# Context keys and values in 512-column products, with the two halves added afterwards

## The chip, the cores and the metric

The kernel runs on one core of one Trainium2 chip. The metric is the device time of one execution in microseconds (us), lower is better. Before the change three runs took 632.14, 632.98 and 632.99 us, median 632.98 us.

## The reference, cut to what matters

One layer: x (1024 tokens by 1024) and a context of 256 tokens by 1024 are normalised and modulated to h and hc. h is multiplied by an input projection of 4096 columns, split into queries, keys, values and gates of an attention half (8 heads of 64) and the parts of a convolution half. Of the context only keys and values are wanted:

```python
kc, vc = jnp.split(hc @ w_in[:, D_ATTN:3 * D_ATTN], 2, axis=-1)
kc = rmsnorm(heads(kc), k_norm_g)
vc = heads(vc)
attn = neighbourhood_attention(q, k, heads(v), kc, vc, rpb) * jax.nn.silu(za)
```

Everything is float32. Both halves are gated, joined, sent through an output projection and added to x.

## The kernel before, in words

To keep precision, each operand of a large product is split into a high part (rounded to the fast matmul type fp32r) and a low part (the rest), and one product becomes three: high by high, high by low, low by high. `mm3` issues these three matmuls into one PSUM accumulator. Tiles that end in h or l, or index 0 and 1, are these parts.

The program has four stages: a start (to about 77 us) that norms and transposes x and the context and makes the first conv columns; the projection of queries, keys and values (to about 267 us); the attention with the other gates' and the conv's products as fillers; and the output projection.

The change lies in the second stage. The loop over n runs over 4 pairs of heads (p) times 8 token tiles (t), with a tail. For a pair, eight chunks of w_in (128 rows by three times 128 columns: the pair's query, key and value columns) are loaded by SyncE (SP) (`chunk_load`) and split (`chunk_split`: ScalarE, ACT, rounds the high part, VectorE, DVE, subtracts for the low part). `proj_tile` multiplies a token tile by the eight chunks, 24 matmuls of 384 columns, into one of four PSUM banks (`pacc`). A step n then runs the later steps of earlier tiles: the root-mean-square scale of tile n-1 (`head_scale`: a square on ACT, a sum on DVE, a power on POOL), its values (`put_v`), then the norm (`normed`, tiles `qn`) and rotary turn (`rotated`, tiles `rot` and `rtmp`) of tile n-2, and the transposes on TensorE (PE) of a pair of tiles (`turn_qk`, tiles `trA` and `trB`).

Once per pair, `ctx_products` multiplies the two context tiles by the key and value columns of the same eight chunks (256 columns), at t = 2 for the first three pairs and at t = 0 for the last. Its two accumulators (`cacc`) take both banks of the PSUM tag U, which the gate and conv units (`pu`) and the gate row (`pgate`) use too. One step later `head_scale` reads them on ACT (`sq<-cacc`), two steps later `normed_ctx` norms the keys (`kn`) and stores the values (`vs<-cacc`), and `turn_kc` transposes the keys (`trC`).

In this stage every engine and SP's queue work strictly in the order of the code: an instruction that waits holds up all that is behind it on its engine. `rtmp` is one buffer (bufs=1).

Of the kernel before, what the change touches and what calls it, by code (L numbers as in the profile page):

```python
# [10 lines left out]
F32 = mybir.dt.float32  # L11
F32R = mybir.dt.float32r
BF16 = mybir.dt.bfloat16
AF = mybir.ActivationFunctionType
ALU = mybir.AluOpType
# [4 lines left out]
P = 128  # L20
# [3 lines left out]
KT = D // P  # L24
# [15 lines left out]
def body(tc, es, x, ctxt, w_ada, b_ada, w_in, q_g, k_g, rpbr, w_out, vecs, cst, out):  # L40
# [21 lines left out]
    pe, act, dve, pool = every = [ordered(e) for e in (nc.tensor, nc.scalar, nc.vector, nc.gpsimd)]  # L62
    sp = ordered(nc.sync)

    def sbuf(name, side=None, bufs=1):
        kw = {} if side is None else {"side": side}
        return tc.tile_pool(name=name, bufs=bufs, reuse_waits="tile", **kw)
# [4 lines left out]
    def mm3(ps, ah, al, bh, bl, first, last):  # L72

        i = pe.matmul(ps, ah, bh, start=first, stop=False)  # L74
        pe.matmul(ps, ah, bl, start=False, stop=False)  # L75
        pe.matmul(ps, al, bh, start=False, stop=last)  # L76
        return i
# [84 lines left out]
    def chunk_load(col, k):  # L162
        raw = wpp.tile([P, 3, P], F32, name="wr", tag="wr", bufs=5)
        chunk_anchor[:] = [sp.dma_start(raw, bass.AP(w_in.tensor, w_in.offset + (k * P) * 4096 + col,
                                                     [[4096, P], [512, 3], [1, P]]))]
        return raw

    def chunk_split(raw):
        raw = raw[:].rearrange("p a b -> p (a b)")
        wh = wpp.tile([P, 384], F32R, name="wh", tag="wh", bufs=12)  # L170
        wl = wpp.tile([P, 384], F32R, name="wl", tag="wl", bufs=12)
        act.copy(wh, raw)
        dve.tensor_tensor(wl, raw, wh[:].bitcast(F32), ALU.subtract)
        return wh, wl

    def load_chunk(col, k):
        return chunk_split(chunk_load(col, k))

    def head_scale(pp, ps, n):

        act.activation(sq[:, :n, :HD], by_head(ps[:, :n * HD]), AF.Square, scale=0.125)
        ss = pp.tile([P, 4], F32, name="ss", tag="ss", bufs=7)
        dve.tensor_reduce(ss[:, :n], sq[:, :n], AX.X, ALU.add)
        pool.tensor_tensor(ss[:, :n], ss[:, :n], mhalf[:, :n], ALU.pow)
        return ss

    def by_head(v):
        return v.rearrange("p (h d) -> p h d", d=HD)
# [7 lines left out]
    def next_vs():  # L196
        vss.append(vss.pop(0))
        return vss[-1]
# [4 lines left out]
    def put_v(vs, i, ps):  # L203

        halves(vs[:, :, 0, i, :HD], vs[:, :, 1, i, :HD], ps.rearrange("p (s d) -> p s d", s=2))
# [50 lines left out]
    def ctx_products(ch):  # L256

        acc = [psm.tile([P, 512], F32, name="cacc", tag="U", bufs=2) for _ in range(2)]
        for k in range(KT):
            wh, wl = ch[k]  # L260
            for i in range(2):
                hk = hc[k // 4][:, k % 4, :, i * P:(i + 1) * P]
                mm3(acc[i][:, :256], hk[:, 0], hk[:, 1],
                    wh[:, P:384], wl[:, P:384], k == 0, k == KT - 1)
        return acc

    def normed_ctx(pp, acc, scales):
        two, vs = [], next_vs()
        for i in range(2):
            qn = pp.tile([P, P], F32, name="kn", tag="kn", bufs=2)  # L270
            normed(qn, acc[i], scales[i], 2)
            pool.tensor_tensor(by_head(qn[:]), by_head(qn[:]), gkc.broadcast_to([P, 2, HD]), ALU.mult)
            put_v(vs, i, acc[i][:, P:256])
            two.append(qn)
        return two, vs
# [13 lines left out]
    def proj_tile(ch, t):  # L289
        ps = bank("pacc", "OOSS"[t % 4])  # L290
        for k in range(KT):
            wh, wl = ch[k]
            mm3(ps[:, :384], hh[k][:, t * P:(t + 1) * P], hl[k][:, t * P:(t + 1) * P], wh, wl, k == 0, k == KT - 1)
        return ps


    def unit_load(col):
        raws = []
        for q in range(2):
            raws.append(uw.tile([P, 4, P], F32, name="uraw", tag="uraw", bufs=2))  # L300
            sp.dma_start(raws[q], w_in[0, q * 512:(q + 1) * 512, col:col + P].rearrange("(k p) n -> p k n", p=P))
        return raws
# [84 lines left out]
    def z_col(f):  # L387
        return CZA + f * P if f < 4 else CZC + (f - 4) * P
# [135 lines left out]
    wpp = wps.enter_context(sbuf("wpp"))  # L524
# [10 lines left out]
    xx, slabs, highs, lows, chunks, mods, pts = {}, {}, {}, {}, {}, {}, {}  # L535
# [171 lines left out]

    def first_columns(half, k, part=range(3)):

        wh, wl = chunks[k]  # L710
        h_, l_ = (v.rearrange("p (b r c) -> p b (r c)", b=8, r=16)[:, :, 64 * half:64 * half + 64]
                  for v in (hh[k], hl[k]))
        for i in part:
            for u in (0, 2, 1):
                uc = slice(u * P, (u + 1) * P)
                pe.matmul(acc0[u][half], (wl if i == 1 else wh)[:, uc], l_ if i == 2 else h_,
                          start=k == 0 and i == 0, stop=k == KT - 1 and i == 2)
# [35 lines left out]
    def split_chunk(k):  # L753
        chunks[k] = chunk_split(chunks[k])
# [70 lines left out]
    for m in range(1, 4):  # L825
        k, new, last = 2 * m, m < 3, m == 3
# [4 lines left out]
        if m == 2:  # L831
            gkc = gains(tables)
            ch = [chunk_load(CQ, k) for k in range(4)]
# [82 lines left out]
    def bank(name, tag):  # L916
        return (pss if tag == "S" else psm).tile([P, 512], F32, name=name, tag=tag, bufs=2)
# [285 lines left out]
    pp = pps.enter_context(sbuf("ppn"))  # L1203
# [12 lines left out]
    def flush():  # L1216
        while stores:
            stores.pop(0)()

    for n in range(NT + 3):  # L1220


        p, t = divmod(n, NB)
        at = 2 if p < NPAIR - 1 else 0
        if 1 <= t and p + 1 < NPAIR:
            raws += [chunk_load(CQ + (p + 1) * P, k) for k in ([t - 1] if t < NB - 1 else [t - 1, t])]
        if n == 0:
            loaded[z_col(4)] = unit_load(z_col(4))
        if n == NT - 8:
            loaded[z_col(0)] = unit_load(z_col(0))  # L1230
        if 1 <= n <= KT:
            gate.load(n - 1)
            next(spread, None)
        if 9 <= n < 25 and n % 2:
            next(tables)
        if n == NT - 3:
            act.activation(few[:, 5:6], ones, AF.Exp)
        if n == NT - 6:
            heads[0].masks()
            heads[0].load_k()  # L1240
        if n == NT - 5:
            heads[0].load_q()
        flush()

        if t == 0 and 0 < n < NT:
            nxt += map(chunk_split, raws)
            ch, nxt, raws = nxt, [], []
        if n == 0:
            next(group0)
        if n == NT - 4:  # L1250
            next(fill)
        if n < NT:
            tiles[n] = proj_tile(ch, t)
        else:
            for _ in range((4, 3, 1)[n - NT]):
                next(fill)
        if 5 <= n < 9:
            for _ in range(2):
                next(group0)
        if n == 9:  # L1260
            for _ in group0:
                pass
        if 0 < n <= NT:
            scales[n - 1] = head_scale(pp, tiles[n - 1], 4)
            if n % 2:
                vs = next_vs()
            put_v(vs, (n - 1) % 2, tiles[n - 1][:, 256:384])
            if n % 2 == 0:
                q, r = divmod(n - 1, NB)
                spill_v(q, r - 1, vs)  # L1270
        if t == at + 1 and n < NT:
            cscales = [head_scale(pp, a, 2) for a in cacc]

        if 1 < n <= NT + 1:
            m, r = n - 2, (n - 2) % NB
            qn = rms_normed(pp, tiles[m], scales.pop(m))
        while waiting:
            waiting.pop(0)()
        if 4 <= t and p + 1 < NPAIR:
            nxt.append(chunk_split(raws.pop(0)))  # L1280
        if 1 < n <= NT + 1:
            tiles[m] = rotated(pp, rope, qn, r)
        if t == at + 2 and n < NT:
            kc = normed_ctx(pp, cacc, cscales)
        do_dves()
        if 2 <= n < KT + 2:
            gate.add(n - 2)
        if 9 <= n < 25 and n % 2 == 0:
            next(tables)
        do_acts()  # L1290

        if n == KT + 3:
            gate.split()
        if n == KT + 5:
            gate.sum()
        if t == at and n < NT:
            cacc = ctx_products(ch)
        if n % 2 == 0 and n >= 4:
            waiting.append(turn_qk(pp, (n - 4) // NB, [tiles.pop(n - 4), tiles.pop(n - 3)], (n - 4) % NB))
        if t == at + 3 and n < NT:  # L1300
            waiting.append(turn_kc(pp, p, *kc))
# [43 lines left out]
    with sbuf("att") as ap, psum("psb") as psb:  # L1345
# [6 lines left out]
        for n in range(4 * NH + 4):  # L1352
# [8 lines left out]
            if ready:  # L1361
                p = ready.pop()
# [153 lines left out]
```

## Time and profile before

| what | value |
|---|---|
| median of three runs | 632.98 us |
| the profiled execution | 632.67 us |
| its span, first to last recorded instruction | 630.9 us |
| PE busy | 624.0 us, 3504 matmuls |
| DVE, ACT busy | 436.8 us, 327.7 us |
| PE in the chain that ended last | 96% |
| products of the context (`cacc`) in that chain | 4% |

The time of the profiled execution is 1.8 us above its span; that rest lies before the first and behind the last recorded instruction. Matmuls overlap in the records, so what a stream of them costs is read from the distance of their starts, which the chain of work shows as the length of a piece over its count, and not from the duration of one.

### The profile page before, as it was taken

What the parts mean: (1) busy time and instruction counts of PE and PEld (TensorE: products, weight loads), DVE (VectorE), ACT (ScalarE), POOL (GpSimd) and SP (SyncE); (2) the same over time, 40 slices, a digit from 0 to 9 for tenths busy, and PEclk for the clock granted to TensorE, in tenths of its full rate; (3) what the DMA queues carried; (4) which work ended last, traced back from release to release, by engine and by line L of the source; (5) the groups of instructions that cost most, each with busy time, mean ns of one, the idle gap of its engine ahead of it and who ended that gap; (6) DMA issues with size and microseconds to landing.
All of it is one profiled execution on the core that took longest, in us unless ns stands there. A gap on an engine that the chain in (4) does not pass through costs nothing.

```text
span 630.9 us, 10022 instructions
## 1 busy us (share of the span) xinstructions
PE 624.0 (99%) x3504; PEld 540.3 (86%) x3504; DVE 436.8 (69%) x866; ACT 327.7 (52%) x705; POOL 77.6 (12%) x102
## 2 busy tenths in 40 slices
PE   8999999999999999999999999999999999999998
PEld 3577899999999999888888888888888888888887
DVE  1887858766856755468888889987998865594211
ACT  4776935424625446346676568567775854460000
POOL 1305014123123222000000000000000002003300
PEclk9999999999999999999999999999999999999999
DMA  8983638866775994975383636673742234962721
GB/s 320 368 284 106 178 114 261 262 199 211 267 244 164 298 330 142 322 230 188 124 290 104 227 94 214 192 272 104 275 124 74 60 101 149 361 210 88 261 101 50
DMA packets 103006, 125.60 MB, mean 199 GB/s; under 512 B 9665, under 2 KB 71577, under 8 KB 101676
## 3 DMA queue, kind: packets, MB, share of 16 engines
q1 hardware_dynamic: 96492, 113.38, 54.4%
q10 hardware_dynamic: 6208, 11.05, 5.5%
q8 instruction: 27, 0.44, 0.3%
q0 software_dynamic: 256, 0.54, 0.3%
q14 instruction: 23, 0.19, 0.1%
HBM read 88.09 MB, written 38.62 MB: 201 GB/s over the span
## 4 chain that ended last, share of the span: by engine, by line
PE 96%; DMA 1%; DVE 1%; SPq 1%; issue 0%; ACT 0%; ACTq 0%
PE pu L55 30%; PE pacc L55 21%; PE po L55 8%; PE acc L55 5%; PE pout L76 5%; PE pout L75 5%; PE pout L74 5%; PE cacc L55 4%; PE tr L55 4%; PE pss L55 3%; PE pmx L55 2%; PE pc L55 2%; DMA xx<-in_x 1%; PE trA L55 1%; PE trB L55 1%
## 5 line engine op out<-in xcount | busy, mean ns | idle before, releaser
L55 PE MATMUL pu<-h,uh 128*128 128x512 f32 x544 | 169.4, 392 | 0.6 <-DVE cv L55 0.6
L55 PE MATMUL pacc<-wh,h 128*128 128x384 f32 x512 | 135.1, 338 | 0.0
L55 PEld LDWEIGHTS pu<-h,uh 128*128 128x128 f32 x544 | 98.1, 188 | 18.2 <-DVE cv L55 1.0
L55 PE MATMUL pu<-h,ul 128*128 128x512 f32 x272 | 106.4, 391 | 0.0
L55 PEld LDWEIGHTS pacc<-wh,h 128*128 128x128 f32 x512 | 92.9, 188 | 0.1
L55 PE MATMUL pacc<-wl,h 128*128 128x384 f32 x256 | 85.6, 334 | 0.0
L55 PEld LDWEIGHTS pu<-h,ul 128*128 128x128 f32 x272 | 51.1, 188 | 11.3
L55 POOL TENSOR_TENSOR ss<-ss,few 128x4 f32<-128x4 f32 (+1 forms) x40 | 41.5, 1038 | 125.2 <-DVE ss L55 125.0
L75 PE MATMUL pout<-wol,yh 128*128 128x512 f32 (+2 forms) x136 | 51.6, 379 | 0.0
L74 PE MATMUL pout<-woh,yh 128*128 128x512 f32 (+2 forms) x136 | 50.5, 379 | 0.0
L76 PE MATMUL pout<-woh,yl 128*128 128x512 f32 (+2 forms) x136 | 49.8, 379 | 0.0
L55 PEld LDWEIGHTS pacc<-wl,h 128*128 128x128 f32 x256 | 48.1, 188 | 0.1
L55 DVE TENSOR_REDUCE ss<-sq 128x4 f32<-128x260 f32 (+1 forms) x40 | 15.7, 393 | 40.6 <-ACT sq L55 40.6
L55 ACT ACTIVATE sq<-pacc 128x256 f32<-128x256 f32 x32 | 12.3, 385 | 52.7 <-PE pacc L55 52.2
L55 DVE TENSOR_REDUCE rm<-pmx 128x2 f32<-128x256 f32 x32 | 13.6, 424 | 30.4 <-PE pmx L55 30.2
L55 DVE TENSOR_TENSOR mx<-mx,sb 128x384 f32<-128x384 f32 (+1 forms) x64 | 33.0, 524 | 2.0
L55 ACT COPY mg<-pmx 128x256 f32<-128x256 f32 x32 | 11.9, 372 | 43.0 <-PE pmx L55 39.9
L55 ACT ACTIVATE qn<-pacc,ss 128x64 f32<-128x64 f32 x128 | 30.1, 330 | 3.0 <-issue 2.5
L55 PE MATMUL po<-phl,v 128*65 128x256 f32 (+2 forms) x160 | 31.3, 291 | 0.0
L55 ACT COPY sc<-pc 128x512 f32<-128x512 f32 x32 | 18.8, 589 | 23.0 <-PE pc L55 22.9
L55 DVE TENSOR_TENSOR pll<-sb,phl 128x768 fp32r<-128x768 f32 (+2 forms) x33 | 28.4, 861 | 1.9 <-ACT sb L55 1.9
L75 PEld LDWEIGHTS pout<-wol,yh 128*128 128x128 f32 x136 | 25.6, 188 | 4.7
(163 smaller groups left out, 1268.7 us busy)
## 6 DMA issues: line engine op xcount, KB each, us to landing
uraw<-in_w_in SPq DMA_DIRECT2D x34, 256.0 KB
q_d<-qs SPq DMA_DIRECT2D x32, 256.0 KB
k_s<-k_d SPq DMA_DIRECT2D x8, 1024.0 KB
q_s<-q_d SPq DMA_DIRECT2D x16, 512.0 KB
wr<-in_w_in SPq DMA_DIRECT2D x40, 192.0 KB
slab<-in_w_ada SPq DMA_DIRECT2D x6, 1024.0 KB
v_d<-vs SPq DMA_DIRECT2D x20, 260.0 KB
v<-v_d SPq DMA_DIRECT2D x16, 325.0 KB
```

Source lines behind the costliest of these rows:

```text
L55: i = emit(*a, **kw)
L74: i = pe.matmul(ps, ah, bh, start=first, stop=False)
L75: pe.matmul(ps, ah, bl, start=False, stop=False)
L76: pe.matmul(ps, al, bh, start=False, stop=last)
```

## The change

`chunk_split` makes one tile of high and low part side by side instead of two tiles, so that a single access pattern can take the key and value columns of both (256 and 256 columns, 384 apart). `ctx_products` then multiplies the context's high part by both at once, 512 columns into a whole PSUM bank (left half: high by high; right half: high by low), and adds the low part by the high weights, 256 columns, into the left half. The new `ctx_sums`, one step later and ahead of `head_scale`, copies the right half to SBUF on ACT, into the buffer `rtmp`, and adds it to the left half on DVE, in PSUM.

```diff
     def chunk_split(raw):
         raw = raw[:].rearrange("p a b -> p (a b)")
-        wh = wpp.tile([P, 384], F32R, name="wh", tag="wh", bufs=12)
-        wl = wpp.tile([P, 384], F32R, name="wl", tag="wl", bufs=12)
+        w = wpp.tile([P, 2, 384], F32R, name="w", tag="w", bufs=12)
+        wh, wl = w[:, 0], w[:, 1]
         act.copy(wh, raw)
-        dve.tensor_tensor(wl, raw, wh[:].bitcast(F32), ALU.subtract)
-        return wh, wl
+        dve.tensor_tensor(wl, raw, wh.bitcast(F32), ALU.subtract)
+        return wh, wl, w[:, :, P:384]
...
         for k in range(KT):
-            wh, wl = ch[k]
+            wh, _, both_ = ch[k]
             for i in range(2):
                 hk = hc[k // 4][:, k % 4, :, i * P:(i + 1) * P]
-                mm3(acc[i][:, :256], hk[:, 0], hk[:, 1],
-                    wh[:, P:384], wl[:, P:384], k == 0, k == KT - 1)
+                pe.matmul(acc[i][:].rearrange("p (l c) -> p l c", l=2), hk[:, 0], both_,
+                          start=k == 0, stop=False, skip_group_check=True)
+                pe.matmul(acc[i][:, :256], hk[:, 1], wh[:, P:384], start=False, stop=k == KT - 1, skip_group_check=True)
         return acc
+
+    def ctx_sums(pp, acc):
+        for a in acc:
+            other = pp.tile([P, 256], F32, name="rtmp", tag="rtmp")
+            act.copy(other, a[:, 256:])
+            dve.tensor_tensor(a[:, :256], a[:, :256], other, ALU.add)
...
         if t == at + 1 and n < NT:
+            ctx_sums(pp, cacc)
             cscales = [head_scale(pp, a, 2) for a in cacc]
```

`proj_tile` and `first_columns` only take the first two of the three values that `chunk_split` now returns.

On PE, at the context's products of pair 0, the order before repeats three matmuls of 256 columns for each of 16 pieces (names: `wh` and `wl` are the parts of the weights, `hc` the context):

```order
L55 MATMUL pacc<-wh,h_766 128x384
L55 MATMUL cacc<-wh,hc 128x256
L55 MATMUL cacc<-wl,hc 128x256
L55 MATMUL cacc<-wh,hc 128x256 x2
L55 MATMUL cacc<-wl,hc 128x256
L55 MATMUL cacc<-wh,hc 128x256 x2
L55 MATMUL cacc<-wl,hc 128x256
```

At the same place it is now two matmuls for each piece (`w` is the tile of both parts):

```order
L55 MATMUL cacc<-w,hc 128x512
L55 MATMUL cacc<-w,hc 128x256
L55 MATMUL cacc<-w,hc 128x512
L55 MATMUL cacc<-w,hc 128x256
L55 MATMUL cacc<-w,hc 128x512
L55 MATMUL cacc<-w,hc 128x256
```

A matmul and its weight load have gone from each piece, 16 of them in a pair and 64 in all, and nothing stands elsewhere on PE.

On ACT, one step later in pair 0, the order before was (tile numbers tell buffers apart):

```order
L55 ACTIVATE sq<-pacc 128x4x64
L55 CAST vs_983<-pacc 128x2x64
L55 ACTIVATE sq<-cacc 128x2x64 x2
L55 ACTIVATE qn<-pacc,ss 128x64 x4
L55 ACTIVATE sq<-pacc 128x4x64
```

Now the same place has two copies ahead of the squares:

```order
L55 ACTIVATE sq<-pacc 128x4x64
L55 CAST vs_967<-pacc 128x2x64
L55 COPY rtmp<-cacc 128x256 x2
L55 ACTIVATE sq<-cacc 128x2x64 x2
L55 ACTIVATE qn<-pacc,ss 128x64 x4
L55 ACTIVATE sq<-pacc 128x4x64
```

The squares and the norm of the tile before (`qn`) have moved behind the copies.

On DVE at that step there are two additions that were not there, behind the low part of tile 2's values and ahead of the sums of squares:

```order
L55 TENSOR_TENSOR rtmp<-qn,rope 128x256
L55 TENSOR_TENSOR rot<-rot,rtmp 128x8x16 x2
L55 SCALAR_TENSOR_TENSOR gacc<-gs,c_125,gacc 128x512 x2
L55 TENSOR_REDUCE ss<-sq 128x4
L55 TENSOR_TENSOR vs_967<-pacc,vs_967 128x2x64
L55 TENSOR_TENSOR cacc<-cacc,rtmp 128x256 x2
L55 TENSOR_REDUCE ss<-sq 128x2 x2
L55 TENSOR_TENSOR rot<-qn,rope 128x256
```

Each copy and each addition wait for the other engine: the first copy for the last reader of `rtmp`, the first addition for the first copy, the second copy for the first addition, the second addition for the second copy.

More of the change, by code (lines that the diff above doesn't have):

```diff
@@ L291, in proj_tile @@
         for k in range(KT):
-            wh, wl = ch[k]
+            wh, wl = ch[k][:2]
             mm3(ps[:, :384], hh[k][:, t * P:(t + 1) * P], hl[k][:, t * P:(t + 1) * P], wh, wl, k == 0, k == KT - 1)
@@ L708, in first_columns @@
     def first_columns(half, k, part=range(3)):
-        wh, wl = chunks[k]
+        wh, wl = chunks[k][:2]
         h_, l_ = (v.rearrange("p (b r c) -> p b (r c)", b=8, r=16)[:, :, 64 * half:64 * half + 64]
```

## The prediction, made before the changed kernel ran

> **What bounds the kernel now.** I read the page first: busy time, clock and the chain that ended last.
>
> ```profile
> span 630.9 us, 10022 instructions
> PE 624.0 (99%) x3504; PEld 540.3 (86%) x3504; DVE 436.8 (69%) x866; ACT 327.7 (52%) x705; POOL 77.6 (12%) x102
> ...
> PEclk9999999999999999999999999999999999999999
> ...
> PE 96%; DMA 1%; DVE 1%; SPq 1%; issue 0%; ACT 0%; ACTq 0%
> ```
>
> PE is busy for 99% of the span, at a granted clock that never leaves the top digit, and it is 96% of the chain. A busy PE could still hide waits, so the second view is the list of what PE waited for, over the whole span.
>
> ```profile
> PE acc L55 <- POOL c L55: 1.4, 1, 1.4
> PE acc L55 <- ACT h L55: 0.8, 1, 0.8
> PE pu L55 <- DVE cv L55: 0.6, 2, 0.5
> PE pmx L55 <- DVE rm L55: 0.5, 1, 0.5
> PE tr L55 <- DVE ab L55: 0.5, 1, 0.5
> PE tr L55 <- DVE rw L55: 0.2, 1, 0.2
> ```
>
> The columns are total us, times and longest. All of it is 1.4 + 0.8 + 0.6 + 0.5 + 0.5 + 0.2 = 4.0 us, and none stands at a `pacc`, `cacc`, `trA` or `trC`, the work of the stage that the change touches. There PE's own instructions are the bound: what they lose in number or length comes off the end, and work on ACT and DVE costs nothing until PE must wait for it. The third view is the chain of work in order of time (start, length, piece and count).
>
> ```profile
> 89.20 5.75 PE cacc L55 x48
> ...
> 103.27 0.22 PE trA L55 x2
> ...
> 108.11 2.77 PE pu L55 x12
> ...
> 141.60 5.75 PE cacc L55 x48
> ...
> 156.35 0.22 PE trA L55 x2
> ...
> 184.50 5.75 PE cacc L55 x48
> ...
> 217.48 5.75 PE cacc L55 x48
> ...
> 261.45 5.46 PE pu L55 x24
> ```
>
> The context's products take 5.75 us in each of the four pairs, 23.0 us in all, or 5.75 / 48 = 0.1198 us for a matmul of 256 columns. `pu` has 512 columns: 2.77 / 12 = 0.2308 us early in the stage and 5.46 / 24 = 0.2275 us late.
>
> **The change, part by part: the products.** A pair had 48 matmuls of 256 columns; it now has 16 of 512 and 16 of 256. The streamed columns are the same: 48 x 256 = 12,288 and 16 x 512 + 16 x 256 = 12,288. Only what a matmul costs beyond its columns can be saved, once for each of the 16 that go. Two matmuls of 256 cost 0.2396 us; one of 512 costs 0.2308 or 0.2275 us. The saving is 0.0088 to 0.0121 us per replaced pair, and with 64 of them 0.56 to 0.77 us. I take **0.7 us**, nearer to the late rows, since their stretch of 24 is the longer one and so less mixed with its ends.
>
> The trace can't show a 512-column matmul whose moving operand is two runs of 256 columns, 384 apart. The nearest row is the start's `acc`, 512 columns of h taken in eight runs of 64:
>
> ```profile
> 75.30 1.39 PE acc L55 x6
> ```
>
> That is 1.39 / 6 = 0.2317 us, 0.0042 us above the late `pu`: the split operand could cost 64 x 0.0042 = 0.27 us. Two runs are fewer than eight, so I count nothing, and keep 0.27 us for the range. Below nothing there is no reason: the columns are the same.
>
> The Trainium skill, "TensorE: Matmul & The Clock Gate", section "Wait — 56ns, not 53.3ns?", gives a fixed cost of about 2.5 ns beyond the columns for each matmul; an estimate by that page is 64 x 2.5 ns = 0.16 us saved. The rows above disagree: 119.8 and 227.5 ns give 2 x 119.8 - 227.5 = 12.1 ns, and the measurement decides.
>
> **The change, part by part: copies and additions.** In each pair two copies of 128x256 from PSUM on ACT and two additions of 128x256 on DVE are new. These groups of the stage stand nearest:
>
> ```profile
> L55 ACT COPY mg<-pmx 128x256 f32<-128x256 f32 x5 | 1.9, 374 | 6.8 <-PE pmx L55 6.2 <-DMA rs_d<-ob 0.6
> ```
>
> ```profile
> L55 DVE TENSOR_TENSOR qs<-trA,qs 128x512 fp32r<-128x512 f32 x16 | 11.0, 690 | 18.2 <-ACT qs L55 18.1
> ...
> L55 DVE TENSOR_TENSOR mx<-pc,sc 128x256 f32<-128x256 f32 x7 | 2.9, 418 | 1.0 <-ACT sc L55 0.9
> ...
> L55 DVE TENSOR_TENSOR vs<-cacc,vs 128x128 fp32r<-128x128 f32 x8 | 1.9, 279 | 0.0
> ```
>
> A copy of this form takes 0.374 us. No row has DVE writing to PSUM; `mx<-pc,sc` has the same size and the same operands (one in PSUM, one in SBUF), so I take 0.418 us, between 0.279 us for half the elements and 0.690 us for twice as many. That is 8 x 0.374 = 3.0 us more on ACT and 8 x 0.418 = 3.3 us more on DVE, off PE's path. What matters is the delay of what queues behind them: on ACT the squares of `cacc` and the norm `qn` of the tile before; on DVE the sums, the rotation `rot` of that tile and the work after it; on PE, in the end, the transposes of `rot`. First pair 1, the cleaner place:
>
> ```profile
> 147.02 0.28 ACT L55 ACTIVATE sq<-cacc 128x128 f32<-128x128 f32 x1 [4.85 <-PE cacc L55]
> 147.79 0.28 ACT L55 ACTIVATE sq<-cacc 128x128 f32<-128x128 f32 x1 [0.49 <-PE trA L55]
> 147.96 0.93 ACT L55 ACTIVATE qn<-pacc,ss 128x64 f32<-128x64 f32 x4
> ```
>
> ```profile
> 147.40 0.29 DVE L55 TENSOR_REDUCE ss<-sq 128x2 f32<-128x130 f32 x1 [3.99 <-ACT sq L55]
> ...
> 151.12 0.49 DVE L55 TENSOR_TENSOR rot<-rot,rtmp 128x128 f32<-128x128 f32 x2
> ```
>
> A hand-over costs 0.10 us: the square ends at 147.30, the sum begins at 147.40. Now the first copy takes the square's place: 147.02 to 147.39; addition 147.49 to 147.91; second copy 148.01 to 148.38; second addition 148.48 to 148.90; sum of the first square 148.90 to 149.19; second square at 149.29; `qn` 0.17 us behind it as before, at 149.46 instead of 147.96. ACT and DVE are **1.5 us late** (1.2 to 2.0 us with the bounds of the addition). The last `rot` then ends at 151.61 + 1.5 = 153.1 us, and the transposes that need it start at 156.35: 3.2 us are left. Pairs 2 and 3 have the same rows with the same distances. In pair 0 DVE is fuller:
>
> ```profile
> 94.62 0.49 DVE L55 TENSOR_TENSOR rot<-rot,rtmp 128x128 f32<-128x128 f32 x2
> ...
> 96.69 0.28 DVE L55 TENSOR_TENSOR vs<-pacc,vs 128x128 fp32r<-128x128 f32 x1
> ...
> 99.49 0.49 DVE L55 TENSOR_TENSOR rot<-rot,rtmp 128x128 f32<-128x128 f32 x2
> ...
> 103.42 0.48 DVE L55 TENSOR_TENSOR vs<-cacc,vs 128x128 fp32r<-128x128 f32 x2
> ```
>
> ```profile
> 97.74 0.92 ACT L55 ACTIVATE qn<-pacc,ss 128x64 f32<-128x64 f32 x4
> ```
>
> The first copy waits for the last reader of `rtmp` (95.11) and is done by 95.6, but its addition stands behind the values, which end at 96.97: addition to 97.39, second copy 97.49 to 97.86, second addition 97.96 to 98.38, sum to 98.67, square at 98.77, `qn` at 98.94 instead of 97.74, **1.2 us late**. The last `rot` ends at 99.98 + 1.2 = 101.2, the transposes start at 103.27: 2.1 us are left. The banks of `cacc` come free when `vs<-cacc` ends at 103.90, late by the same 1.2 us at most, and the next user, `pu`, starts at 108.11. So all of it is hidden, and I count **nothing**; if that cover went, each us beyond it would be one of PE's.
>
> **Tiles and queues.** The one weight tile has the two tiles' bytes and number of buffers, the order of `chunk_split` is unchanged, and no DMA is added. SP's loads are strictly ordered, and those that wait for DVE (gate weights behind `gacc`) can slip by the same 1.2 us; no wait of PE for a DMA stands in the list above. I count nothing.
>
> **The sum.** Against the profiled execution, 632.67 us (its span and 1.8 us around it): 632.67 - 0.7 = **632.0 us**, 0.1% less. The median of the runs shown is 0.3 us above that execution, so a median of new runs would by the same sum be 632.3 us.
>
> **The rivals.** (1) *Weight loads set the pace of the narrow matmuls.* Then taking 64 loads away frees more than the fixed cost. A row speaks for it: the 128-column matmuls at the end.
>
> ```profile
> 625.78 0.27 PE L76 MATMUL pout<-woh,yl 128*128 128x128 f32 x1
> ...
> 627.79 0.28 PE L76 MATMUL pout<-woh,yl 128*128 128x128 f32 x1
> ```
>
> The first and last of 19 in a row: 2.01 / 18 = 0.112 us for half the columns of a `cacc`, so something other than columns holds the narrow ones. If it held `cacc` too, and a 256 behind a 512 ran free of it, a piece would cost the difference by columns: (0.2275 - 0.1198) = 0.108 us for 256, so 0.2275 + 0.108 = 0.335 us against 3 x 0.1198 = 0.359 us. That saves 64 x 0.024 = 1.5 us, 631.1 us. Against it: 0.1198 is above that floor, and it is just the step that columns and a fixed cost of 12 ns give. The Trainium skill, the same page, section "Back-to-back issue gap", says that the spacing in a stream of loads and matmuls is set by both; by that rule this rival holds. Its figures, 81 ns at 128 columns and 131 ns at 512, fit no row here (112 and 227.5 ns).
>
> (2) *PE waits for the late rotation* (slower). The two copies and additions hand over `rtmp` four times, the last to the sums. It decides from a delay of 3.29 us in pair 0 (99.98 to 103.27) and 4.74 us in the others (151.61 to 156.35). If each hand-over took 1 us more than the 0.10 us seen, the delays would be 5.2 and 5.5 us, PE would lose 1.9 + 3 x 0.8 = 4.3 us, and the time would be 632.0 + 4.3 = 636.3 us. Against it: hand-overs of 0.10 us, and 2.1 us still free in the tightest pair. For it: DVE is in order and full around pair 0.
>
> (3) *The saving does not reach the end.* PE comes to the attention 0.7 us earlier and waits there for what it found ready before, so the end stays at 632.7 us. Against it: PE's waits in and after the attention's start are 1.1 us in all (`pmx`, `pu`), and both hang on work that starts from PE.
>
> **How the numbers follow.** About 0.2% (1.3 us) is what a measurement of this kernel can tell from no change. My forecast has 0.72, rival (3) 0.08, both inside that; rival (1) 0.08, faster by 0.24%; rival (2) 0.12, slower. So faster 0.08, same 0.80, slower 0.12. The range takes in (1) and (3), the split operand's 0.27 us, the spread of the three runs (0.85 us) and a first us of a stall: 630.9 to 633.4 us.
>
> **What would show it.** Right: the chain has pieces of `cacc` x32 of 5.55 to 5.62 us where x48 took 5.75; ACT has copies of about 0.37 us and DVE additions of about 0.42 us; `qn` behind them starts 1.2 to 1.5 us later against the end of `cacc`; PE's list of waits has no new row. Wrong: a piece of `cacc` under 5.45 us (rival 1), a wait of PE at `trA` for DVE `rot` (rival 2), a longer wait in the attention (rival 3), or a 512-column `cacc` that takes well over 0.232 us.

## The result, and the profile after

The changed kernel takes 631.9 us (median of 22 runs, 631.35 to 633.25) against 633.13 us before (22 runs beside it). The ratio is 0.998 with a 95% interval of 0.9974 to 0.9987: faster by 0.13 to 0.26%, 1.2 us between the medians. The profiled execution takes 632.35 us with a span of 630.6 us. The prediction was 632.0 us, in a range of 630.9 to 633.4 us, with a gain of 0.7 us.

The chain of work after the change, read as before: start, length, piece and count.

```profile
77.25 12.48 PE pacc L55 x72
89.73 5.55 PE cacc L55 x32
...
103.60 0.22 PE trA L55 x2
...
108.44 2.77 PE pu L55 x12
...
141.92 5.55 PE cacc L55 x32
...
156.46 0.22 PE trA L55 x2
...
184.63 5.55 PE cacc L55 x32
...
217.43 5.55 PE cacc L55 x32
...
267.33 0.24 PE pss L55 x2
```

All four pieces of `cacc` have gone from 5.75 to 5.55 us: 4 x 0.20 = 0.80 us. Before, the stage began with its first `pacc` and ended with the first `pss` of the attention at these times:

```profile
76.69 12.51 PE pacc L55 x72
...
267.57 0.24 PE pss L55 x2
```

That is 190.88 us before and 267.33 - 77.25 = 190.08 us after: the stage is 0.80 us shorter, as much as the four pieces. From `pss` to the end of the span it is 630.9 - 267.57 = 363.3 us before and 630.6 - 267.33 = 363.3 us after. The start of the program, ahead of the first `pacc`, took 0.56 us longer in the profiled execution after the change; that is why the two spans differ by 0.3 us only.

What PE waited for after the change (total, times, longest):

```profile
PE acc L55 <- POOL c L55: 1.4, 1, 1.4
PE acc L55 <- ACT h L55: 0.8, 1, 0.8
PE pu L55 <- DVE cv L55: 0.6, 2, 0.4
PE pmx L55 <- DVE rm L55: 0.5, 1, 0.5
PE tr L55 <- DVE xss L55: 0.2, 1, 0.2
PE acc L55 <- issue: 0.2, 1, 0.2
```

No row has come in the stage of the change. The new work stands on ACT and DVE; first pair 1 in the timeline of ACT, then that of DVE.

```profile
147.16 0.37 ACT L55 COPY rtmp<-cacc 128x256 f32<-128x256 f32 x1 [4.66 <-PE cacc L55]
148.09 0.37 ACT L55 COPY rtmp<-cacc 128x256 f32<-128x256 f32 x1 [0.56 <-PE trA L55]
...
149.32 0.92 ACT L55 ACTIVATE qn<-pacc,ss 128x64 f32<-128x64 f32 x4
```

```profile
147.57 0.43 DVE L55 TENSOR_TENSOR cacc<-cacc,rtmp 128x256 f32<-128x256 f32 x1 [3.83 <-ACT rtmp L55]
148.50 0.43 DVE L55 TENSOR_TENSOR cacc<-cacc,rtmp 128x256 f32<-128x256 f32 x1 [0.49 <-ACT rtmp L55]
...
152.48 0.49 DVE L55 TENSOR_TENSOR rot<-rot,rtmp 128x128 f32<-128x128 f32 x2
```

The copies and additions alternate, as the one buffer demands. The bracket on the second copy names a transpose on PE, but the copy starts as the first addition ends (147.57 + 0.43 = 148.00), which is its real releaser. The norm `qn` starts at 149.32 instead of 147.96, while PE's piece of `cacc` ended 0.13 us later: 1.2 us of delay. The rotation ends at 152.97, 3.5 us before the transposes at 156.46 take it.

In pair 0 the norm, on ACT, and the end of the rotation, on DVE:

```profile
98.72 0.92 ACT L55 ACTIVATE qn<-pacc,ss 128x64 f32<-128x64 f32 x4
```

```profile
100.47 0.49 DVE L55 TENSOR_TENSOR rot<-rot,rtmp 128x128 f32<-128x128 f32 x2
```

The norm starts at 98.72 instead of 97.74 us, 1.0 us later, with the end of `cacc` 0.33 us later (95.28 against 94.95). The rotation ends at 100.96, 2.6 us before the transposes at 103.60.

### The profile page after: what moved, and what is told of

It reads as the page before. It is cut to its first block, busy times and chain, and to the rows that moved or that the text cites. A ratio compares the mean times of both kernels' runs of the same rounds, so it can differ in the third digit from the quotient of the medians.

```text
span 630.6 us, 9908 instructions
## 1 busy us (share of the span) xinstructions
PE 624.0 (99%) x3439; PEld 537.1 (85%) x3440; DVE 439.1 (70%) x874; ACT 330.0 (52%) x713; POOL 77.6 (12%) x102
## 4 chain that ended last, share of the span: by engine, by line
PE 98%; DVE 1%; issue 0%; POOL 0%; ACT 0%; POOLq 0%
PE pu L55 30%; PE pacc L55 21%; PE po L55 8%; PE acc L55 6%; PE tr L55 5%; PE pout L75 5%; PE pout L76 5%; PE pout L74 5%; PE cacc L55 4%; PE pss L55 3%; PE pmx L55 2%; PE pc L55 2%; PE trA L55 1%; PE trB L55 1%; POOL xss L55 0%
## 5 line engine op out<-in xcount | busy, mean ns | idle before, releaser
L55 PE MATMUL pacc<-w,h 128*128 128x384 f32 x768 | 138.4, 337 | 0.0
L55 PEld LDWEIGHTS pacc<-w,h 128*128 128x128 f32 x768 | 132.7, 188 | 0.2
L55 PE MATMUL acc<-h,w 128*128 128x512 f32 x144 | 38.1, 404 | 0.8 <-ACT h L55 0.8
L55 PEld LDWEIGHTS acc<-h,w 128*128 128x128 f32 x144 | 25.5, 188 | 6.5 <-ACT h L55 1.2
L74 PEld LDWEIGHTS pout<-woh,yh 128*128 128x128 f32 x136 | 25.6, 188 | 4.7
```

What stands on the lines that cost most here:

```text
L55: i = emit(*a, **kw)
```

## The experiments

The theory: a matmul costs its columns and a fixed part, 64 matmuls have gone and with them their fixed part, and the sums are hidden. Rivals: the rest of the change (one tile, or what the sums move) makes or takes part of the time; a delay of ACT and DVE costs PE at once; something other than a fixed part holds narrow matmuls. Beside each time stands that of the kernel before on the same chip.

### The changed kernel again

The same code, as the measure of the spread.

> The changed kernel once more, beside the next three on the same chip. Theory (fixed cost of a matmul): each pair's context products take 5.55 us instead of 5.75, so from the first pacc to the first pss of the attention the kernel is 0.8 us shorter than before, and so is its time: 0.8 us or 0.13% less than before. If the 1.2 us between the medians is all the change's own work, a second part of 0.4 us must show at another place of the trace, the same in each profile.

Measured: 632.38 us against 633.06 us, ratio 0.9987 (0.9978 to 0.9996), 0.7 us between the medians. Its profile:

```profile
77.23 12.51 PE pacc L55 x72
89.74 5.55 PE cacc L55 x32
...
267.34 0.24 PE pss L55 x2
```

The stage takes 190.11 us. No second part of the gain shows, in this profile or the one before it. The traces say 0.8 us; the two ratios, 0.8 to 1.6 us and 0.3 to 1.4 us with their intervals, allow that, the first at its lower edge. The 0.4 us that the first median shows beyond 0.8 was not found in a trace. What does differ from profile to profile is the start: in the profiles of before, of after and of every experiment whose first `pacc` is given here, that `pacc` stands between 76.56 and 78.04 us, whatever the kernel.

### The one weight tile alone

```diff
-            wh, _, both_ = ch[k]
+            wh, wl = ch[k][:2]
...
-                pe.matmul(acc[i][:].rearrange("p (l c) -> p l c", l=2), hk[:, 0], both_,
-                          start=k == 0, stop=False, skip_group_check=True)
-                pe.matmul(acc[i][:, :256], hk[:, 1], wh[:, P:384], start=False, stop=k == KT - 1, skip_group_check=True)
+                mm3(acc[i][:, :256], hk[:, 0], hk[:, 1],
+                    wh[:, P:384], wl[:, P:384], k == 0, k == KT - 1)
...
-            ctx_sums(pp, cacc)
```

> Only the one weight tile of the change; the context's products are the three of 256 columns as before, and there are no sums. Theory: 5.75 us of cacc in each pair, and the time of before within the spread (0 +- 0.3 us). Rival (the common tile gives the part of the gain that the products don't): 0.4 us less than before.

Measured: 632.8 us against 633.06 us, ratio 0.9993 (0.9984 to 1.0001): no difference that can be told. The stage in its profile:

```profile
76.56 12.51 PE pacc L55 x72
89.07 5.75 PE cacc L55 x48
...
267.44 0.24 PE pss L55 x2
```

It takes 190.88 us, as before to the hundredth. The tile gives nothing that the stage shows.

### The 512-column product as two of 256

```diff
-                pe.matmul(acc[i][:].rearrange("p (l c) -> p l c", l=2), hk[:, 0], both_,
-                          start=k == 0, stop=False, skip_group_check=True)
+                for l in range(2):
+                    pe.matmul(acc[i][:, 256 * l:256 * l + 256], hk[:, 0], both_[:, l],
+                              start=k == 0 and l == 0, stop=False, skip_group_check=True)
```

> The changed kernel with each 512-column product issued as two of 256 columns into the two halves of the bank; the copies and additions stay. Theory: 48 matmuls in each pair again, 5.75 us of cacc, and 0.8 us more than the changed kernel, so the time of before although 6.4 us of copies and additions are in it. Rival (the sums or the tile make the difference, not the number of matmuls): the time of the changed kernel.

Measured: 632.92 us against 633.06 us, ratio 0.9996 (0.9987 to 1.0005). The stage:

```profile
78.04 12.50 PE pacc L55 x72
90.54 5.75 PE cacc L55 x48
...
268.91 0.24 PE pss L55 x2
```

190.87 us: with the number of matmuls back, the gain is gone, although tile, copies and additions are all there. So it is the number of matmuls that the change is worth, and the sums cost nothing. Each matmul that goes takes its weight load along (3440 loads after the change, 3504 before and here), so the fixed part is that of the two together; no run separates them.

### Without the sums

Only the call of `ctx_sums` is left out; the context's keys and values then lack their high by low products.

```diff
-            ctx_sums(pp, cacc)
```

> The changed kernel without the copies and additions, so that the high by low products of the context are left out of its keys and values. Theory (the sums are hidden under PE): the time of the changed kernel, no difference that can be measured. Rival (the sums take some of the gain): less than the changed kernel, by up to the 1.4 us per pair by which they delay ACT and DVE.

Measured: 631.78 us against 633.06 us, ratio 0.9981 (0.9972 to 0.999). Its stage runs from 76.89 to 266.99, 190.10 us, against 190.08 and 190.11 us with the sums. The median lies 0.12 us below the lower of the changed kernel's own two (631.9 and 632.38), which differ by more than that themselves.

### Two and six more copies and additions

```diff
             dve.tensor_tensor(a[:, :256], a[:, :256], other, ALU.add)
+        for n in range(2):
+            a = acc[n % 2]
+            other = pp.tile([P, 256], F32, name="rtmp", tag="rtmp")
+            act.copy(other, a[:, 256:])
+            dve.tensor_tensor(a[:, 256:], a[:, 256:], other, ALU.add)
```

> Behind the sums of each pair stand two more copies and additions of the same kind, on the right halves of the banks, whose values nobody reads any more. A copy and an addition take 0.93 us with their hand-overs in the trace after the change, so ACT and DVE are 1.9 us later than in the changed kernel. The rotation is ready 2.6 us (pair 0) and 3.5 to 3.7 us (the others) before PE's transposes need it. Theory (hidden up to that distance): the time of the changed kernel. Rival (delays of ACT and DVE cost part of their length at once): some us more.

Measured: 632.21 us against 632.87 us, ratio 0.999 (0.9981 to 0.9999). The norm in pair 1 starts at 150.93 us, with PE 0.13 us earlier than after the change: 1.7 us later than there. The stage takes 267.20 - 77.10 = 190.10 us. A delay of about 3 us in all, that of the change included, is still hidden.

With `range(6)`:

> The same with six more copies and additions in each pair: 5.6 us of delay. Theory (beyond the distance each us is one of PE's): PE waits 5.6 - 2.6 = 3.0 us in pair 0, 2.1, 2.1 and 1.9 us in the others, at the transposes behind rot; 9 us more than the changed kernel, about 641 us. Rival (the delay is taken up elsewhere, such as by idle ACT and DVE): little or nothing more.

Measured: 644.43 us against 632.87 us, ratio 1.0169 (1.0152 to 1.0187), 12 us more than the kernel with two. PE's list of waits has three new rows:

```profile
PE trA L55 <- DVE rot L55: 5.4, 4, 2.8
PE trC L55 <- DVE qs L55: 1.9, 2, 1.0
...
PE trA L55 <- DVE qs L55: 0.8, 3, 0.3
```

The first is the wait of rival (2), once in each pair, 2.8 us in pair 0 (3.0 expected) and about 0.9 us in the others (1.9 to 2.1 expected). There, other transposes wait too, for the banks that `qs` is copied out of. The list gives 8.1 us together, but it counts only the time in which no matmul shows, and the ends of matmuls are modelled. The starts show more of the same wait in pair 0:

```profile
104.45 0.27 PE L55 MATMUL trB<-ci,rot 128*128 128x128 f32 x1
107.55 0.33 PE L55 MATMUL trA<-ci,rot 128*128 128x128 f32 x1 [2.83 <-DVE rot L55]
```

From start to start pass 3.1 us, where the transposes before stand 0.11 us apart: 3.0 us lost. A second cost is the clock: the granted clock in the stretches around this wait, from the windows (PE, PEld, DVE, ACT and POOL busy, then PEclk).

```profile
100.00:104.00 4.00, 4.00 (x25) 4.00 (x24) 2.16 (x5) 1.53 (x5) 0.00 (x0) 1.00 0.80 264
```

```profile
104.70:107.50 2.80, 0.03 (x1) 0.00 (x0) 1.89 (x8) 2.42 (x12) 1.36 (x2) 1.00 0.26 77
107.90:109.90 2.00, 2.00 (x11) 2.00 (x10) 2.00 (x6) 1.64 (x8) 0.66 (x1) 0.69 0.29 74
109.90:112.00 2.10, 2.10 (x8) 2.10 (x8) 2.07 (x7) 0.61 (x4) 2.10 (x3) 0.50 0.73 241
112.00:114.00 2.00, 2.00 (x13) 1.96 (x12) 2.00 (x5) 1.59 (x6) 1.03 (x2) 0.98 0.62 166
```

The clock did not fall in the wait itself but behind it: narrower windows still show 1.00 from 108.3 to 108.6 us, 0.50 from 108.9 to 112.0 us, and 0.93 from 112.0 to 112.5 us. So PE worked again for 1.1 us at full clock and then ran at half clock for 3.4 us. In 109.90 to 112.00 stand 8 matmuls, and 13 stand two us later. The tile behind the wait shows the price, in the chain:

```profile
108.10 5.75 PE pacc L55 x24
...
116.84 4.17 PE pacc L55 x24
```

5.75 - 4.17 = 1.6 us. The waits of 0.9 us in the other pairs left the clock at 1.00.

The starts account for the whole. Both kernels have 3439 matmuls in the trace in the same order, so each one's start can be set beside its start in the kernel with two. The distance grows by 3.0 us at pair 0's wait and by 1.6 us in the stretch at half clock. At the transposes `trA` and `trB` of pairs 1, 2 and 3 it grows by 1.7 us each, and at `trC` of pairs 1 and 2 by 1.2 and 1.1 us. That is 12.0 us.

Only one of the five runs kept its clock: it shows a mean of 1.000 and took 641.79 us, the other four show 0.997 and took 643.93 to 645.1 us. In a span of 643 us, 3.4 us at half clock make just that 0.997. So behind waits as this kernel has them the clock fell in four executions and not in the fifth; of that one there is no trace, so how long PE waited in it is not known.

The Trainium skill, "TensorE: Matmul & The Clock Gate", section "What's actually happening", says that the array falls back to half clock after an idle window of about 3.4 us. The half clock agrees; the idle time that sufficed here is 2.8 us by the row, and in one run of five the clock stayed up.

### Narrow products

```diff
-                pe.matmul(acc[i][:, :256], hk[:, 1], wh[:, P:384], start=False, stop=k == KT - 1, skip_group_check=True)
+                for j in range(2):
+                    pe.matmul(acc[i][:, j * P:j * P + P], hk[:, 1], wh[:, P + j * P:2 * P + j * P],
+                              start=False, stop=k == KT - 1 and j == 1, skip_group_check=True)
```

> The changed kernel with each 256-column product of the context's low part issued as two of 128 columns: 64 matmuls more. If a matmul costs its columns and a fixed 12 ns, two of 128 take 2 x 66 ns and the kernel is 64 x 12 ns = 0.8 us slower than the changed one. If something else holds narrow matmuls at 0.112 us, as the last ones of the output projection show, two take 0.224 us where one took 0.120, and it is 64 x 0.104 = 6.7 us slower.

Measured: 639.1 us against 632.87 us, ratio 1.0096 (1.0082 to 1.011), 6.9 us more than the kernel with two more copies, measured beside it.

```profile
77.43 12.51 PE pacc L55 x72
89.93 7.25 PE cacc L55 x48
...
274.44 0.24 PE pss L55 x2
```

A piece of `cacc` takes 7.25 us, 1.70 us more; four give 6.8 us. With 0.227 us for each 512-column product, 32 of 128 columns take 7.25 - 16 x 0.227 = 3.62 us, 0.113 us each. That is a mean: by the starts, 0.28 us pass from the 512-column product to the first of 128, 0.06 us to the second, and 0.11 us to the next 512. So two rules describe the sums: down to 256 columns a matmul costs its columns and 12 to 13 ns; an added one of 128 columns costs 0.113 us, hardly less than one of 256. The first is the change's gain, the second is no part of it. What holds the narrow ones, their weight loads or something else, no run here separates.

### The last output tile, cut evenly or not at all

The last output tile is made in pieces of 384 and 128 columns, so that the addition and transfer behind the last matmul are small. The narrow ones cost more than was known, so this is a version that might beat both.

```diff
-        pieces = [slice(0, 384), slice(384, 512)] if (nh, t) == (1, NB - 1) else [slice(0, 512)]
+        pieces = [slice(0, 256), slice(256, 512)] if (nh, t) == (1, NB - 1) else [slice(0, 512)]
```

> The changed kernel with its last output tile cut into 256 and 256 columns instead of 384 and 128. Theory (128-column matmuls are held at 0.112 us): 24 x (0.174 + 0.112) = 6.9 us of PE become 24 x 2 x 0.120 = 5.8 us, 1.1 us less; the addition behind the last matmul has 256 columns instead of 128, about 0.13 us more. So 1.0 us less than the changed kernel, if the last transfer is no longer for its size. Rival (narrow matmuls cost by their columns): 24 x (0.174 + 0.066) = 5.8 us both ways, and the time of the changed kernel or a little more.

Measured: 631.37 us against 632.74 us, ratio 0.9976 (0.9965 to 0.9986). The last addition in the chain, here and in the changed kernel:

```profile
626.39 0.42 DVE ot L1451
```

```profile
627.80 0.29 DVE ot L1451
```

With the first `pss` at 267.00 here and at 267.33 there, it starts 359.39 and 360.47 us behind `pss`: 1.1 us earlier, and takes 0.13 us longer. From `pss` to the end of the span it is 629.4 - 267.0 = 362.4 us instead of 363.3 us, 0.9 us less.

With one piece, `[slice(0, 512)]` for all:

> The same with the last tile in one piece of 512 columns: 24 x 0.227 = 5.4 us of PE, 1.4 us less, but the addition behind the last matmul is 0.69 us instead of 0.29. Theory: 1.0 us less than the changed kernel, as much as with two even pieces, less what the larger last transfer costs.

Measured: 631.81 us against 632.74 us, ratio 0.9984 (0.9975 to 0.9992). Its span ends 630.0 - 267.2 = 362.8 us behind `pss`, 0.5 us less than the changed kernel:

```profile
626.40 0.69 DVE L1451 TENSOR_TENSOR ot<-pout,xr 128x512 f32<-128x512 f32 x1 [4.75 <-PE pout L76]
627.12 0.33 SPq L1452 DMA_DIRECT2D out<-ot  x1
```

The addition takes 0.4 us longer than that of 128 columns, and from the issue of the last transfer to the end of the span pass 630.0 - 627.1 = 2.9 us; in the changed kernel 630.6 - 628.1 = 2.5 us. Two even pieces are the best of the three. Their medians, 631.37 and 631.81 us, lie 0.5 and 0.1 us below the lower of the changed kernel's own two, which differ by 0.5 us themselves and were not measured beside these; what is shown is the 0.9 and 0.5 us in the trace.

## Why the prediction was right

- **The bound.** PE's own instructions set the stage: its 0.80 us is that of the four pieces of `cacc`, and the sums' 6.4 us show nowhere in it (`two_halves`, `no_sums`).
- **The products.** Forecast 0.7 us, between 0.56 and 0.77 us by rows; it is 0.80 us, or 12.5 ns for each matmul that went, a little above the rows' 8.8 to 12.1 ns. The mechanism is the forecast one, a fixed part for each matmul (with its load). Only the sum of a pair is a price: 5.55 / 16 = 0.347 us for 512 and 256 columns together. With 0.1198 us for the 256, the 512 would cost 0.227 us, as the late `pu` rows said; the distances of the starts are 0.230 and 0.117 us, so the division is not shown. The two runs of 256 columns cost nothing extra that shows.
- **Copies and additions.** Forecast 0.374 and 0.418 us; measured 0.37 and 0.43 us. The forecast delay of 1.5 us in pair 1 is 1.2 us. From copy to addition pass 0.04 us, not 0.10, twice (147.53 to 147.57, 148.46 to 148.50); the sum of squares starts 0.09 us before the record of the second addition ends, and the second square 0.03 us behind that sum. In pair 0 the delay is 1.0 us where 1.2 was forecast, and only 0.65 us against the end of `cacc`, so the sign "1.2 to 1.5 us later against the end of `cacc`" came true in pairs 1 to 3 (1.2 us each) and not in pair 0. That DVE wrote to PSUM here made no difference to speak of: 0.43 us, against 0.418 us to SBUF.
- **Tiles and queues.** Nothing counted, and `tile_only` shows nothing.
- **Rival (1), weight loads.** It did not hold: it asked for 0.335 us for a 512 with its 256, or pieces of 5.36 us; the pieces are 5.55 us, 0.347 us for the two. The 0.112 us row on which it rested is real, but holds narrower matmuls only (`narrow`).
- **Rival (2), the late rotation.** It did not come true in the change, and the distances of 2.6 and 3.5 us fit as the threshold: 1.9 us more cost nothing, and 5.6 us more cost PE 3.0 us at pair 0's rotation, which is 5.6 - 2.6. At the rotations of the others it cost 1.7 us, somewhat less than 5.6 - 3.5 = 2.1. The price beyond the distance, one us for one us in the prediction, was too low in all (12.0 us for 9): `trC` is held up too (2.3 us), and the long wait is followed by a lower clock (1.6 us).
- **Rival (3), the gain lost behind.** It did not hold: 363.3 us from `pss` to the end both times.
- **The sum.** 632.0 us forecast for the profiled execution and 632.3 us for a median of new runs; measured 632.35 us, and medians of 631.9 and 632.38 us. That these lie so near is partly luck: the medians of one kernel differ by 0.5 us between two sets of runs. Of the gain itself, the first set shows 1.2 us (0.8 to 1.6), just above the forecast 0.7 us, and the second 0.7 us; the 0.80 us of the stage is the firmer figure.

## What to carry to other kernels

Where TensorE is the bound, count matmuls as well as columns: here each one that goes, with its weight load, is worth 12.5 ns, so widening is a gain that can be estimated beforehand and is small, and 128-column pieces cost nearly as much as 256. Work moved to other engines is free up to the distance between its result and PE's use of it; read that distance in the timeline before, and stay well inside it, since beyond it more than the excess was lost here (12 us for 9). For changes under 0.3%, compare the length of the changed stage in the traces: here it repeats to 0.03 us, while medians move by 0.5 us.

## What the runs showed of the hardware that was not expected

In streams of this type, each matmul with its weight load, one of 128 columns takes 0.112 to 0.113 us on average, one of 256 takes 0.120, one of 384 takes 0.174 and one of 512 takes 0.227 us (the late `pu` rows). After a wait of 2.8 us in `more6` the clock stayed at 1.00 for the first 1.1 us of work and then fell to 0.50 for 3.4 us. By the mean clocks, that happened in four runs of five. It did not fall behind waits of 0.9 us.
